# Three kinds of small extra products in the MLPs' first product, and one placement for all operands

## The chip, the cores and the metric

The kernel runs on one core of a Trainium2 chip. The number to predict is the device time of one execution, in microseconds (us). Engines are named as the profile does: PE is TensorE (PEld its weight loads), DVE is VectorE, ACT is ScalarE, POOL is GpSimd, SP is SyncE, which issues the weight DMAs. "Product" below is one matmul instruction.

## The reference

Three transformer-like layers over 256 tokens of width 1024, all in float32. The first block mixes three branches (a sparse attention, a gated recurrence, a short convolution); the second block has two layers, each with two kinds of attention. Every layer ends with the same kind of MLP:

```python
def squared_relu_mlp(h, w_up, w_down):
    return jnp.square(jax.nn.relu(h @ w_up)) @ w_down

x = x + squared_relu_mlp(rmsnorm(x, norm_mlp[layer]), w_up[layer], w_down[layer])
```

`w_up` is 1024 x 4096 and `w_down` 4096 x 1024, so an MLP's first product has 32 output tiles of 128 rows with 8 steps over the inner dimension. There are three MLPs: that of the first block, and one in each layer of the second.

## The kernel before, in words

Activations are kept transposed, features on partitions and the 256 tokens in the free dimension. A float32 product is made of three products in the one-pass type fp32r: weights and activations are each split into a high part and a rest, and high x high, high x rest and rest x high are added up in PSUM. The method `gemm` (lines 250, 253 and 254) issues these three for each step k, 128 x 128 weights stationary and 256 tokens moving. Weights come as one stream through SP; for each unit of 8 blocks ACT writes the high part `whi` (L193) and DVE the rest `wlo` in two pieces (L195).

The activations' two parts lie in one tile `xo`. Where they begin in it is set per stage by the table `PLACES`, in elements of 4 bytes; the tile itself begins at a multiple of 128 bytes plus 64. `HIDDEN` does the same for the MLP's hidden tile `hid`, which begins at a multiple of 128 bytes.

`residual` adds the last projection to x tile by tile (L375 on DVE), writes the next operand (L326 on ACT, L327 on DVE) and sums the squares of x on POOL (L339, L340) except the last, which ACT squares (L342). `mlp` begins with `variance`: two exact float32 products with a matrix of ones (`sum_squares`, L347 and L348) into the pool `po`, which has a single buffer, then a scaling by DVE that reads it (L382) and a reciprocal (L383). The mean square is not needed before the MLP's second product: the first product does not wait for it. In the first product each of 16 rounds makes two output tiles (`gemm2`: two calls of `gemm`, 24 products each); L395 to L398 make the squared ReLU. The second product runs mostly as pairs of one product of 512 columns and one of 256 (`gemm_wide`, L262 and L263), 7 tiles of 32 pairs for each MLP, and one last tile by `gemm`.

A scheduler orders each engine's instructions from the dependencies and its own estimates; the engines then run their queues in that order. `after(a, b)` adds an order between two instructions of one engine.

Of the kernel before, what the change touches and what calls it, by code (L numbers as in the profile page):

```python
# [10 lines left out]
FP32 = mybir.dt.float32  # L11
# [30 lines left out]


ROOM = 128
PLACES = {"block1": 32, "ln_mlp_g": 64, "norm_mix0": 24, "norm_mlp0": 96, "norm_mix1": 20, "norm_mlp1": 0}
HIDDEN = {"norm_mix0": 16, "norm_mix1": 48, None: 8}
MIXED = 16
HEADS = [16, 112]

# [33 lines left out]
def kernel(  # L83
# [11 lines left out]
    nc = tc.nc  # L95
    nosync = mybir.DependencyInfo(mybir.DependencyClass.NoSync, mybir.DependencyReason.DATA)

    def after(first, last):
        if last is not None:
            tc.add_manual_dep(first.ins, last.ins.name, nosync)  # L100

    def pool(name, bufs=1, space=None, stack=ctx):
        kw = {"space": space} if space is not None else {}
        return stack.enter_context(tc.tile_pool(name=name, bufs=bufs, **kw))
# [9 lines left out]
    po_p = pool("po", 1, PSUM)  # L114
# [7 lines left out]
    def placed(t, n, at):  # L122

        return t[:, at:at + n * T].rearrange("p (k t) -> p k t", k=n)

    def place(stage):

        nonlocal xh, xl
        at = PLACES[stage]
        xh, xl = placed(xo, KD, at), placed(xo, KD, at + KD * T)  # L130
# [3 lines left out]
    cst = keep.tile([128, NCONST], FP32, name="cst")  # L134
    ones = keep.tile([128, 128], FP32, name="ones")
# [10 lines left out]
    a = 0  # L146
    for k, cols in ((2, slice(0, FIRST)), (5, slice(FIRST, UW)), (8, slice(UW, CW))):
# [3 lines left out]
        a = e  # L151
# [16 lines left out]
    def v_(name, j=0):  # L168
        o = VOFF[name][0] + j
        return vec[:, o:o + 1]  # L170
# [5 lines left out]
    units = {}  # L176
# [6 lines left out]
    def take(u, pieces=2):  # L183

        c, i = divmod(u, CHUNK_UNITS)
        if c not in staged:
            load(c)
        src = staged[c][:, i * UW:(i + 1) * UW]
        h = whi_p.tile([128, UW], FP32R, name="whi")
        l = wlo_p.tile([128, UW], FP32R, name="wlo")  # L190
        n = UW // pieces
        pieces = [slice(q * n, (q + 1) * n) for q in range(pieces)]
        act = [nc.scalar.activation(out=h[:, z], in_=src[:, z], func=AF.Copy)  # L193
               for z in (pieces if u == 0 else [slice(0, UW)])]
        dve = [nc.vector.tensor_tensor(out=l[:, z], in0=src[:, z], in1=h[:, z], op=ALU.subtract) for z in pieces]  # L195
        chain = hold.pop(0) if hold else None
        if chain:
            after(act[0], chain[0])
            after(dve[0], chain[1])
        units.clear()  # L200
        units[u] = h, l

    def block(n=1):

        b = stream["block"]
        stream["block"] = b + n
        u, i = divmod(b, UNIT)
        assert i + n <= UNIT
        if u not in units:
            take(u)  # L210
        h, l = units[u]
        return h[:, i * 128:(i + n) * 128], l[:, i * 128:(i + n) * 128]
# [18 lines left out]
    def slot(steps=1):  # L231
        for d in list(due):
            d[0] -= 1
            if d[0] <= 0:
                due.remove(d)
                d[1]()
        credit[0] = credit[0] + steps if chains else 0
        while credit[0] >= 1:
            credit[0] -= 1
            step()  # L240

    def drain():
        while due or chains:
            slot()

    def gemm(ps, ks, ah, al, prev=None):

        for k in ks:
            h, l = block()
            m0 = nc.tensor.matmul(out=ps, lhsT=h, rhs=ah[:, k], start=(k == ks[0]), stop=False)  # L250
            if k == ks[0]:
                after(m0, prev)
            nc.tensor.matmul(out=ps, lhsT=h, rhs=al[:, k], start=False, stop=False)  # L253
            m1 = nc.tensor.matmul(out=ps, lhsT=l, rhs=ah[:, k], start=False, stop=(k == ks[-1]))  # L254
        return m1

    def gemm_wide(kt, a):

        ps = pg_p.tile([128, 2, T], FP32, name="pg")
        for k in range(kt):  # L260
            h, l = block()
            nc.tensor.matmul(out=ps, lhsT=h, rhs=a[:, k], start=(k == 0), stop=False)  # L262
            nc.tensor.matmul(out=ps[:, 1], lhsT=l, rhs=a[:, k, 0], start=False, stop=(k == kt - 1))  # L263
        slot(kt / KD)
        return ps

    def gemm1(kt, ah, al, steps=1):
        ks = kt if isinstance(kt, range) else range(kt)
        ps = pg_p.tile([128, 2, T], FP32, name="pg")
        gemm(ps[:, 0], ks, ah, al)  # L270
        slot(steps * len(ks) / KD)
        return ps[:, 0]

    def gemm2(kt, ah, al):
        ps = pg_p.tile([128, 2, T], FP32, name="pg")
        m = gemm(ps[:, 0], range(kt), ah, al)
        gemm(ps[:, 1], range(kt), ah, al, prev=m)
        slot(2 * kt / KD)
        return ps
# [44 lines left out]
    def operand(j, gain):  # L324

        nc.scalar.activation(out=xh[:, j], in_=x[:, j], func=AF.Copy, scale=v_(gain, j))  # L326
        nc.vector.scalar_tensor_tensor(out=xl[:, j], in0=x[:, j], scalar=v_(gain, j), in1=xh[:, j],  # L327
                                       op0=ALU.mult, op1=ALU.subtract)
# [16 lines left out]
    def sum_squares():  # L345
        ps = po_p.tile([128, 2, T], FP32, name="po")
        nc.tensor.matmul(out=ps[:, 0], lhsT=ones, rhs=sqa, start=True, stop=False)  # L347
        nc.tensor.matmul(out=ps[:, 0], lhsT=ones, rhs=sq_last["s"], start=False, stop=True)  # L348
        return ps[:, 0]
# [29 lines left out]
    def mlp(gain_next):  # L379
        def variance():  # L380
            u = tmp.tile([128, 512], FP32, name="rs_u", bufs=1)[:, 0:T]
            nc.vector.tensor_scalar(out=u, in0=sum_squares(), scalar1=1.0 / D, scalar2=EPS, op0=ALU.mult, op1=ALU.add)  # L382
            nc.vector.reciprocal(out=rvar, in_=u)  # L383

        variance()
        with ExitStack() as st:
            hp = pool("hid", stack=st)
            mp = pool("mlpt", 2, stack=st)
            hid = hp.tile([128, FF // 128 * 2 * T + ROOM], FP32R, name="hid")
            hid = placed(hid, FF // 128 * 2, HIDDEN[gain_next]).rearrange("p (k i) t -> p k i t", i=2)  # L390
            for j in range(0, FF // 128, 2):
                ps = gemm2(KD, xh, xl)
                r = mp.tile([128, 2, T], FP32, name="r")
                s = mp.tile([128, 2, T], FP32, name="s")
                nc.scalar.activation(out=r, in_=ps, func=AF.Relu)  # L395
                nc.scalar.activation(out=hid[:, j:j + 2, 0], in_=r, func=AF.Square)
                nc.vector.scalar_tensor_tensor(out=s, in0=ps, scalar=0.0, in1=r, op0=ALU.max, op1=ALU.mult)
                nc.vector.tensor_tensor(out=hid[:, j:j + 2, 1], in0=s, in1=hid[:, j:j + 2, 0], op=ALU.subtract)  # L398
            if gain_next is not None:
                place(gain_next)  # L400
            for j in range(KD):

                wide = j < KD - WN
                if wide:
                    ps = gemm_wide(FF // 128, hid)
                else:
                    ps = gemm1(FF // 128, hid[:, :, 0], hid[:, :, 1])

                for z in HALVES if gain_next is None and j == KD - 1 else [slice(0, T)]:
                    t = tmp.tile([128, T], FP32, name="dn")[:, z]  # L410
                    if wide:
                        nc.scalar.activation(out=t, in_=ps[:, 1], func=AF.Copy)
                        nc.vector.tensor_tensor(out=t, in0=ps[:, 0], in1=t, op=ALU.add)
                    nc.vector.tensor_tensor(out=t, in0=t if wide else ps[:, z], in1=rvar[:, z], op=ALU.mult)  # L414
                    nc.vector.tensor_tensor(out=x[:, j, z], in0=t, in1=x[:, j, z], op=ALU.add)  # L415
                    if z.stop - z.start < T:
                        nc.scalar.activation(out=rstd[:, z], in_=x[:, j, z], func=AF.Square)  # L417
                if gain_next is not None:
                    operand(j, gain_next)
                    squares(j)  # L420
                else:
                    if j < KD - 1:
                        squares(j)
                    nc.scalar.activation(out=xg[:, j], in_=x[:, j], func=AF.Copy, scale=v_("norm_final", j))  # L424
# [460 lines left out]
    for turn in (4096.0, 1.0):  # L885
# [4 lines left out]
        for i in range(6):  # L890
            m, e = math.frexp(rest)
# [14 lines left out]
    with ExitStack() as st:  # L906
# [82 lines left out]
        for j in range(0, 8, 2):  # L989
# [4 lines left out]
            qk(f"e{j + 1}")  # L994
        residual(oh, ol, GROUPS_ATT, "norm_mlp0")
    mlp("norm_mix1")


    first(rsqrt(sum_squares(), T, 1.0 / D, rstd))
    with ExitStack() as st:  # L1000
# [97 lines left out]
        a, b = rope(kr, 32)  # L1098
# [4 lines left out]
        for j in range(2):  # L1103
# [3 lines left out]
            a, b = rope(zr, 128)  # L1107
# [26 lines left out]
    room = pool("room").tile([128, 6, T // 2], FP32, name="room")  # L1134
# [213 lines left out]
```

## Time and profile before

| what | value |
|---|---|
| median of 2 runs | 1079.78 us (1079.7 to 1079.85) |
| the profiled execution's own time | 1079.46 us |
| its span, first to last instruction | 1077.7 us |
| PE busy | 1055.1 us, 98% of the span, 8136 products |
| DVE, ACT, POOL busy | 836.2, 602.0, 158.8 us |
| granted TensorE clock, mean | 0.998 |

An exact float32 product shows as two records of PE. Products are pipelined: each is shown some 0.28 us long while the next one starts after little more than a third of that, so what a product costs is read from the distance between starts, not from its length. A window's count includes products that were already running at its left edge.

### The profile page before, as it was taken

What the parts mean: (1) busy time and instruction counts of PE and PEld (TensorE: products, weight loads), DVE (VectorE), ACT (ScalarE), POOL (GpSimd) and SP (SyncE); (2) the same over time, 40 slices, a digit from 0 to 9 for tenths busy, and PEclk for the clock granted to TensorE, in tenths of its full rate; (3) what the DMA queues carried; (4) which work ended last, traced back from release to release, by engine and by line L of the source; (5) the groups of instructions that cost most, each with busy time, mean ns of one, the idle gap of its engine ahead of it and who ended that gap; (6) DMA issues with size and microseconds to landing.
All of it is one profiled execution on the core that took longest, in us unless ns stands there. A gap on an engine that the chain in (4) does not pass through costs nothing. (4 is left out here: it accounts for less than half of the span.)

```text
span 1077.7 us, 20317 instructions
## 1 busy us (share of the span) xinstructions
PE 1055.1 (98%) x8136; PEld 1015.3 (94%) x8136; DVE 836.2 (78%) x1613; ACT 602.0 (56%) x944; POOL 158.8 (15%) x174
## 2 busy tenths in 40 slices
PE   7999999999999999999999999999999999999996
PEld 7999989999999988899999999888999999999886
DVE  8999898887996666678778866667689788666663
ACT  6467456665575544456654655444458755555441
POOL 1045650110500001120003000011121022000110
PEclk9999999999999999999999999999999999999999
DMA  8544333545455555554433555554444334555541
GB/s 319 201 170 159 132 118 132 182 173 185 157 199 193 196 186 179 185 209 151 148 136 139 189 175 186 196 192 163 169 181 157 118 118 170 185 193 196 186 166 40
DMA packets 29007, 183.94 MB, mean 171 GB/s; under 512 B 3056, under 2 KB 6384, under 8 KB 7280
## 3 DMA queue, kind: packets, MB, share of 16 engines
q1 hardware_dynamic: 28768, 182.50, 47.5%
q8 instruction: 64, 1.05, 0.4%
q14 instruction: 31, 0.25, 0.1%
q10 hardware_dynamic: 144, 0.13, 0.0%
HBM read 181.57 MB, written 1.05 MB: 169 GB/s over the span
## 5 line engine op out<-in xcount | busy, mean ns | idle before, releaser
L195 DVE TENSOR_TENSOR wlo<-stg,whi 128x512 fp32r<-128x512 f32 (+1 forms) x676 | 470.8, 737 | 164.7 <-ACT whi L193 158.4
L193 ACT ACTIVATE whi<-stg 128x1024 fp32r<-128x1024 f32 (+1 forms) x340 | 356.0, 1050 | 333.8 <-PE pg L253 184.9
L250 PE MATMUL pg<-xo,whi 128*128 128x256 f32 x1472 | 415.7, 283 | 7.5 <-ACT whi L193 6.5
L254 PE MATMUL pg<-xo,wlo 128*128 128x256 f32 x1472 | 415.0, 282 | 0.4 <-DVE wlo L195 0.3
L253 PE MATMUL pg<-xo,whi 128*128 128x256 f32 x1472 | 414.4, 282 | 0.6 <-DVE xo L327 0.6
L250 PEld LDWEIGHTS pg<-xo,whi 128*128 128x128 f32 x1472 | 276.6, 188 | 8.9 <-ACT whi L193 6.8
L254 PEld LDWEIGHTS pg<-xo,wlo 128*128 128x128 f32 x1472 | 278.8, 190 | 1.7 <-DVE wlo L195 1.1
L253 PEld LDWEIGHTS pg<-xo,whi 128*128 128x128 f32 x1472 | 276.9, 188 | 2.1 <-DVE xo L327 1.3
L262 PE MATMUL pg<-hid,whi 128*128 128x512 f32 x672 | 235.1, 394 | 0.0
L263 PE MATMUL pg<-hid,wlo 128*128 128x256 f32 x672 | 188.9, 281 | 0.0
L262 PEld LDWEIGHTS pg<-hid,whi 128*128 128x128 f32 x672 | 126.3, 188 | 28.8
L263 PEld LDWEIGHTS pg<-hid,wlo 128*128 128x128 f32 x672 | 126.3, 188 | 0.0
L335 POOL TENSOR_TENSOR sqa<-xv 128x256 f32<-128x256 f32 x6 | 4.1, 677 | 468.3 <-DVE xv L415 302.8
L339 POOL TENSOR_TENSOR sq<-xv 128x256 f32<-128x256 f32 x36 | 28.3, 791 | 174.7 <-DVE xv L415 170.8
L289 PE MATMUL pg<-whi,xo 128*128 128x256 f32 x256 | 47.5, 283 | 0.0
L289 PEld LDWEIGHTS pg<-whi,xo 128*128 128x128 f32 x256 | 39.5, 188 | 0.1
L479 ACT ACTIVATE p<-p,m 128x128 f32<-128x128 f32 x64 | 28.6, 448 | 18.3 <-DVE m L477 18.3
L340 POOL TENSOR_TENSOR sqa<-sqa,sq 128x256 f32<-128x256 f32 x36 | 36.6, 1017 | 2.4
L253 PE MATMUL pg<-ol,whi 128*128 128x256 f32 x128 | 36.4, 286 | 0.2 <-DVE ol L299 0.2
L398 DVE TENSOR_TENSOR hid<-s,hid 128x512 fp32r<-128x512 f32 x48 | 33.2, 691 | 4.0
L254 PE MATMUL pg<-oh,wlo 128*128 128x256 f32 x128 | 36.1, 285 | 0.0
L289 PE MATMUL pg<-wlo,xo 128*128 128x256 f32 x128 | 36.0, 281 | 0.0
(356 smaller groups left out, 1540.1 us busy)
## 6 DMA issues: line engine op xcount, KB each, us to landing
stg<-w SPq DMA_DIRECT2D x168, 1024.0 KB, 4.8
t<-t_bias SPq DMA_DIRECT2D x8, 128.0 KB, 2.5
cb<-chk_bias SPq DMA_DIRECT2D x1, 1024.0 KB, 4.8
xv<-x_in SPq DMA_DIRECT2D x2, 384.0 KB, 5.9
cst<-consts SPq DMA_DIRECT2D x1, 640.0 KB, 10.6
stg<-w SPq DMA_DIRECT2D x1, 512.0 KB, 7.7
out<-xg SPq DMA_DIRECT2D x2, 256.0 KB, 2.5
stg<-w SPq DMA_DIRECT2D x1, 384.0 KB, 6.4
```

The source lines that it names most:

```text
L193: act = [nc.scalar.activation(out=h[:, z], in_=src[:, z], func=AF.Copy) for z in (pieces if u == 0 else [slice(0, UW)])]
L195: dve = [nc.vector.tensor_tensor(out=l[:, z], in0=src[:, z], in1=h[:, z], op=ALU.subtract) for z in pieces]
L250: m0 = nc.tensor.matmul(out=ps, lhsT=h, rhs=ah[:, k], start=(k == ks[0]), stop=False)
L253: nc.tensor.matmul(out=ps, lhsT=h, rhs=al[:, k], start=False, stop=False)
L254: m1 = nc.tensor.matmul(out=ps, lhsT=l, rhs=ah[:, k], start=False, stop=(k == ks[-1]))
L262: nc.tensor.matmul(out=ps, lhsT=h, rhs=a[:, k], start=(k == 0), stop=False)
L263: nc.tensor.matmul(out=ps[:, 1], lhsT=l, rhs=a[:, k, 0], start=False, stop=(k == kt - 1))
L289: nc.tensor.matmul(out=ps, lhsT=a[:, k, t], rhs=w_, start=(k == 0 and i == 0), stop=(k == kt - 1 and i == 2))
L339: nc.gpsimd.tensor_tensor(out=s, in0=x[:, j], in1=x[:, j], op=ALU.mult)
L340: nc.gpsimd.tensor_tensor(out=sqa, in0=sqa, in1=s, op=ALU.add)
L398: nc.vector.tensor_tensor(out=hid[:, j:j + 2, 1], in0=s, in1=hid[:, j:j + 2, 0], op=ALU.subtract)
L479: nc.scalar.activation(out=p[:, a:b], in_=p[:, a:b], func=AF.Exp, scale=-1.0, bias=m[:, i:i + 1], accum_out=sums[:, i:i + 1])
```

## The change

Before the first step of each of the 32 calls of `gemm` in an MLP's first product, one to three extra products are issued into a tile of the pool `po`, whose result nobody reads. Their kind depends on the MLP. In the first ("tokens") the activations are stationary and n columns of weights move; 8 entries in turn, 11 products, so 44 in all. In the second ("dense") the weights are stationary and n tokens move: 32 products. In the third ("exact") ones and constants in plain float32: 32 products. All of `PLACES` becomes 32 and all of `HIDDEN` 8, so that `xo` operands begin 64 bytes past a multiple of 128 in every stage (they did in four of six) and `hid` 32 bytes past one (it did in the third MLP, and 64 past it in the first two).

```diff
-PLACES = {"block1": 32, "ln_mlp_g": 64, "norm_mix0": 24, "norm_mlp0": 96, "norm_mix1": 20, "norm_mlp1": 0}
-HIDDEN = {"norm_mix0": 16, "norm_mix1": 48, None: 8}
+PLACES = {"block1": 32, "ln_mlp_g": 32, "norm_mix0": 32, "norm_mlp0": 32, "norm_mix1": 32, "norm_mlp1": 32}
+HIDDEN = {"norm_mix0": 8, "norm_mix1": 8, None: 8}
+
+BETWEEN = {
+    "norm_mix0": [("tokens", 256), ("tokens", 256, 2), ("tokens", 128), ("tokens", 256, 3),
+                  ("tokens", 240), ("tokens", 200), ("tokens", 248), ("tokens", 136)],
+    "norm_mix1": [("dense", n) for n in (72, 88, 104, 120, 100, 68, 84, 92, 76, 108, 116, 124, 136, 152, 8, 24)],
+    None: [("exact", n) for n in (1, 16, 64, 100, 128, 200, 248, 256)],
+}
...
+    between = {"list": [], "n": 0, "room": None}
+
+    def small(ah, prev):
+
+        kind, n, times = (between["list"][between["n"] % len(between["list"])] + (1,))[:3]
+        between["n"] += 1
+        h = next(iter(units.values()))[0]
+        for _ in range(times):
+            a, b = {"tokens": (ah[:, 0, 0:128], h[:, 0:n]), "dense": (h[:, 0:128], ah[:, 0, 0:n]),
+                    "exact": (ones, cst[:, 0:n])}[kind]
+            m = nc.tensor.matmul(out=between["room"][:, 0:n], lhsT=a, rhs=b, start=True, stop=True)
+            after(m, prev)
+            prev = m
+        return prev
+
     def gemm(ps, ks, ah, al, prev=None):
 
         for k in ks:
             h, l = block()
+            if k == ks[0] and between["list"]:
+                prev = small(ah, prev)
             m0 = nc.tensor.matmul(out=ps, lhsT=h, rhs=ah[:, k], start=(k == ks[0]), stop=False)
             if k == ks[0]:
                 after(m0, prev)
...
+            between.update(list=BETWEEN[gain_next], n=0, room=po_p.tile([128, 512], FP32, name="po"))
             for j in range(0, FF // 128, 2):
                 ps = gemm2(KD, xh, xl)
...
+            between["list"] = []
```

The extra lines also move what follows: lines ahead of 250 are 7 higher in the changed kernel (L195 becomes L202), later ones 24 to 26 (L250, L253, L254 become L274, L277, L278; L327, L375 become L351, L399; L347, L348 become L371, L372; L382, L383 become L406, L407; the extra product is L263).

PE at the start of the second MLP, before. `oh`, `ol` are the operands of the last residual tile, `xo` those of the MLP's first product:

```order
L250 MATMUL pg<-oh,whi 128x256
L253 MATMUL pg<-ol,whi 128x256
L254 MATMUL pg<-oh,wlo 128x256
L250 MATMUL pg<-xo,whi 128x256
L253 MATMUL pg<-xo,whi 128x256
L254 MATMUL pg<-xo,wlo 128x256
```

The MLP's first tile follows the residual's last tile directly. The two sums of squares stand some 70 rows further on, among later tiles of the same product:

```order
L250 MATMUL pg<-xo,whi 128x256
L253 MATMUL pg<-xo,whi 128x256
L347 MATMUL po<-sqa,ones 128x256
L348 MATMUL po<-sq,ones 128x256
L254 MATMUL pg<-xo,wlo 128x256
```

The same place in the changed kernel, with what each waits for left out:

```order
L274 MATMUL pg<-oh,whi 128x256
L277 MATMUL pg<-ol,whi 128x256
L278 MATMUL pg<-oh,wlo 128x256
L371 MATMUL po<-sqa,ones 128x256
L372 MATMUL po<-sq,ones 128x256
L263 MATMUL po<-xo,whi 128x72
L274 MATMUL pg<-xo,whi 128x256
```

The extra product needs the buffer of `po`, so both sums of squares, and DVE's read of them, now stand ahead of the first tile; it stands so in all three MLPs.

DVE at the same place, before (L327 are the rests of the operand, L195 the weights' rests):

```order
L375 TENSOR_TENSOR xv<-pg,xv 128x256
L195 TENSOR_TENSOR wlo<-stg,whi 128x512 x2
L327 SCALAR_TENSOR_TENSOR xo<-xv,xo 128x256 x3
L195 TENSOR_TENSOR wlo<-stg,whi 128x512 x2
L382 TENSOR_SCALAR rs_u<-po 128x256
L383 RECIPROCAL rvar<-rs_u 128x256
```

And in the changed kernel:

```order
L399 TENSOR_TENSOR xv<-pg,xv 128x256
L202 TENSOR_TENSOR wlo<-stg,whi 128x512 x2
L351 SCALAR_TENSOR_TENSOR xo<-xv,xo 128x256 x3
L406 TENSOR_SCALAR rs_u<-po 128x256
L407 RECIPROCAL rvar<-rs_u 128x256
```

The read of the sums moves one pair of L195 forward; what stands ahead of it is unchanged. In the first MLP the order up to the read is that of before, with the angle arithmetic of L884 to L899 behind it.

## Rows read from the trace of the kernel before

**Rows 1.** The page's first part: busy time, share of the span, instructions of PE.

```profile
PE 1055.1 (98%) x8136; PEld 1015.3 (94%) x8136; DVE 836.2 (78%) x1613; ACT 602.0 (56%) x944; POOL 158.8 (15%) x174
```

**Rows 2.** Stretches: window, length, busy time (xcount) of each engine, PEclk, DMA share, GB/s.

```profile
32.00:46.00 14.00, 14.00 (x126) 14.00 (x126) 14.00 (x47) 5.66 (x6) 0.00 (x0) 1.00 0.56 202
290.00:360.00 70.00, 70.00 (x597) 70.00 (x596) 55.47 (x99) 44.05 (x55) 0.00 (x0) 1.00 0.56 196
384.00:450.00 66.00, 66.00 (x380) 57.81 (x379) 44.51 (x71) 29.46 (x36) 9.00 (x11) 1.00 0.54 192
686.00:752.00 66.00, 66.00 (x376) 57.29 (x375) 43.77 (x71) 28.43 (x35) 8.96 (x11) 1.00 0.52 188
986.00:1050.00 64.00, 64.00 (x371) 56.72 (x371) 40.73 (x65) 28.61 (x35) 8.49 (x10) 1.00 0.51 181
```

**Rows 3.** Timeline of PE around exact products: start, length, engine, line, operation.

```profile
289.19 0.59 PE L348 MATMUL po<-sq,ones 128*128 128x256 f32 x2
289.43 0.47 PE L250 MATMUL pg<-xo,whi 128*128 128x256 f32 x1
289.73 0.28 PE L253 MATMUL pg<-xo,whi 128*128 128x256 f32 x1
...
475.51 0.50 PE L360 MATMUL sc<-cst,rstd 128*128 128x1 f32 x4
475.87 0.49 PE L289 MATMUL pg<-whi,xo 128*128 128x256 f32 x2
476.19 0.28 PE L289 MATMUL pg<-wlo,xo 128*128 128x256 f32 x1
```

**Rows 4.** Timeline at the first MLP's start, PE, ACT and DVE.

```profile
283.50 0.29 PE L254 MATMUL pg<-mh,wlo 128*128 128x256 f32 x1
...
288.54 0.40 ACT L342 ACTIVATE sq<-xv 128x256 f32<-128x256 f32 x1
...
289.81 0.34 DVE L884 TENSOR_SCALAR sq<-sq,xv 128x256 f32<-128x256 f32 x1
```

**Rows 5.** Timeline at the second MLP's start, PE, DVE and POOL.

```profile
585.57 0.28 PE L254 MATMUL pg<-oh,wlo 128*128 128x256 f32 x1
...
591.88 2.59 DVE L327 SCALAR_TENSOR_TENSOR xo<-xv,xo 128x256 fp32r<-128x256 f32 x3
...
592.40 1.79 POOL L340 TENSOR_TENSOR sqa<-sqa,sq 128x256 f32<-128x256 f32 x2
```

**Rows 6.** Timeline at the third MLP's start, PE and POOL.

```profile
886.18 0.28 PE L254 MATMUL pg<-oh,wlo 128*128 128x256 f32 x1
...
892.63 2.06 POOL L340 TENSOR_TENSOR sqa<-sqa,sq 128x256 f32<-128x256 f32 x2
```

**Rows 7.** Stretches, instructions of `xo` alone: PE, PEld, DVE, ACT, clock, DMA.

```profile
283.63:290.60 6.97, 6.18 (x46) 5.58 (x47) 2.27 (x4) 1.02 (x2) 1.00 0.51 162
585.69:595.70 10.01, 9.25 (x72) 8.78 (x73) 5.34 (x7) 1.53 (x3) 1.00 0.29 105
886.30:896.15 9.85, 9.24 (x73) 8.74 (x74) 5.54 (x7) 1.52 (x4) 1.00 0.18 57
```

**Rows 8.** The end: PE's last product, and two stretches (columns as Rows 2).

```profile
1069.35 0.39 PE L1145 MATMUL sc<-rstd,ones 128*128 128x128 f32 x2
...
1069.80:1073.00 3.20, 0.00 (x0) 0.00 (x0) 3.05 (x12) 0.77 (x4) 0.00 (x0) 1.00 0.00 0
1073.00:1074.00 1.00, 0.00 (x0) 0.00 (x0) 1.00 (x2) 0.00 (x0) 0.00 (x0) 0.77 0.85 257
```

**Rows 9.** Timeline of PE at the kernel's start.

```profile
5.01 0.58 PE L250 MATMUL pg<-xo,whi 128*128 128x256 f32 x1 [5.01 <-ACT whi L193]
...
11.42 0.41 PE L250 MATMUL pg<-xo,whi 128*128 128x256 f32 x1
11.63 0.41 PE L253 MATMUL pg<-xo,whi 128*128 128x256 f32 x1
...
12.04 0.28 PE L250 MATMUL pg<-xo,whi 128*128 128x256 f32 x1
```

## Prediction

> **What bounds the kernel.** I read the busy shares first: PE works in 98% of the span, so the time is PE's stream of products plus its few idle places, and whatever is put into that stream or holds it up is paid in full [rows 1]. Then stretches, to see what a product costs: in the first MLP's first product 70 us hold 597 products; two were already running at the left edge, so one starts every 70/595 = 0.1176 us [rows 2]. The reader should see in the same rows that this spacing isn't fixed: an early stretch of the first block, with the same product at the same offset, gives 14.00/124 = 0.1129 us. The second products show it too. A pair (512 and 256 columns) takes 66/189 = 0.3492 us in the first MLP, 66/187 = 0.3529 in the second, both with `hid` at 64 bytes, and 64/184.5 = 0.3469 in the third, at 32. The granted clock is 1.00 in all five. So there are at least two paces at 64 bytes. Last I read timelines where the changed kernel has a new order: the three starts of an MLP [rows 4 to 6].
>
> **Extra products.** The exact kind has rows. From the start of L348 to that of the second product behind it 0.54 us pass, less one ordinary 0.118: an exact product of 256 columns costs 0.422 us [rows 3]. Two of one column (L360, four records) and two ordinary ones take 476.19 - 475.51 = 0.68 us; less 2 x 0.118 that is 0.444, so 0.222 for one, 0.111 for a record: a floor, whatever the width. I take the larger of 0.222 and 0.422 x n/256. The eight widths then cost 5 x 0.222 + 0.330 + 0.409 + 0.422 = 2.27 us, four times over **9.1 us**.
>
> Of fp32r no row shows fewer than 256 columns. 24 of the "tokens" products have 256 and cost 24 x 0.118 = 2.8 us. The other 20, and all 32 "dense" ones, cost at least a record's floor, 52 x 0.111 = 5.8 us. At most they run at the exact type's rate of 0.422/256 = 1.65 ns a column: the 20 have 4 x 952 columns, 6.3 us, and the dense ones, with the floor under the two narrowest, 5.2 us, together 11.5. The fp32r row alone speaks for the low end; but that these products are narrow is just what no row covers, so I take the middle, 8.6 us. All 108 products: 9.1 + 2.8 + 8.6 = **20.5 us**, between 17.7 and 23.4. None is hidden: PE is full around each of them.
>
> **The start of each MLP.** The extra products' buffer comes from the pool `po`, which has one. It is free once VectorE has read the sums of squares (L382, now L406), so in PE's queue both sums and that read stand ahead of the MLP's first tile. Before, PE worked on tiles in this time. Behind the waiting product the whole first product is queued, and PE has nothing else.
>
> When can PE go on? In the second MLP, POOL's last addition ends at 592.40 + 1.79 = 594.19; VectorE's last operand at 591.88 + 2.59 = 594.47, which is in time [rows 5]. The two sums follow: the second starts 0.42 later and runs 0.59 as L348 did [rows 3], to 595.2; the read takes about 0.4 (an estimate from the 0.34 of a VectorE operation of the same width [rows 4]). PE goes on near 595.7, having finished the residual at 585.57 + 0.28 = 585.85 [rows 5]. In the third MLP POOL ends at 894.69, so PE goes on near 896.15, after 886.46 [rows 6]. In the first MLP ScalarE's square ends at 288.94, and the sum is over near 289.6; but VectorE first works through L884, to 290.15, so PE goes on near 290.6, after 283.79 [rows 4].
>
> The loss is the tile work done before in these windows: 46, 72 and 73 products [rows 7], at 0.1176 us 5.4, 8.5 and 8.6 us. In the second and third windows the kernel before had not yet run its two sums (2 x 0.42 = 0.84); the changed one has, so 0.84 comes off each. Net 5.4 + 7.6 + 7.7 = **20.8 us** (18.5 to 23). Nothing gives it back: ScalarE and VectorE get ahead, but PE wasn't waiting for them. This work gets no cover elsewhere.
>
> **The clock.** After PE's last product, over at 1069.74, the granted clock is still 1.00 until 1073 and 0.77 as a mean of the next microsecond [rows 8]: it fell to its lower level (1.2 of 2.4 GHz) some 3.7 us after work ended. The new gaps before the sums in the second and third MLP are 594.19 - 585.85 = 8.3 and 894.69 - 886.46 = 8.2 us, so it will fall there. At the low level products start 0.21 us apart (11.63 less 11.42), and at the kernel's start it took from 5.01 to about 11.85 until they got short [rows 9]. So each of the two gaps costs 0.84 for sums at half pace, and up to 4.5 us of products at 0.21 instead of 0.118, up to 2.0 us. I take 1.0 of it: 2 x 1.84 = **3.7 us**. The first MLP's gap is broken after 3.1 us by the first sum, and I put 0 there. Ends: 0 (no fall) and 7.7 (all three in full).
>
> **Paces.** Every extra product disturbs the stream, and behind it a tile of 24 may run at the slow pace or the fast one. All three first products, 3 x 768 = 2,304 products, at the fast pace would give back 2,304 x 4.7 ns = 10.8 us; the other end is 0. No row says which follows a disturbance; I take a quarter, **-2.7 us**. The second products' `hid` at 32 bytes should run like the third MLP's: 224 pairs x (2.3 + 6.0) ns = 1.9 us; since 64 bytes has two paces, 32 may have a slower one too (3.7 ns a pair, as at 64), which would make it +0.6. I take **-1.5**. Some 1,030 products of the two attention layers move from other offsets to 64: by the two paces between -4.8 and +1; I take **-0.5**.
>
> Against these terms stands a rule of the Trainium skill, "TensorE: Matmul & The Clock Gate", in "Step-by-step: what each phase is for": PE has two independent read ports into SBUF, so loading the next weights takes nothing from the running product. By it offsets should not matter, and the sum would be 4.7 us higher. The trace doesn't agree with it as a full account, since pace differs at one clock and one width [rows 2]; whether the ports cause that no row shows.
>
> **Sum.** 20.5 + 20.8 + 3.7 - 2.7 - 1.5 - 0.5 = 40.3. The profiled execution took 1079.46, so 1119.8; the median of the runs is 0.3 higher: **1120 us**, 3.7% slower. The order in which the remaining VectorE work stands (the angle arithmetic comes earlier in the first MLP, L195 later by one pair elsewhere) I cost at nothing: five buffers for each part of the weights let ScalarE and VectorE run ahead of PE. If that cover is gone, a late unit costs PE a wait of at most one unit, 24 products or 2.8 us.
>
> **Rivals.**
> - *Fast pace everywhere.* Each extra product resets the stream to the fast pace. For: both paces occur at 64 bytes. Against: the slow one held through 597 products. It gives 10.8 - 2.7 = 8 us more and up to 4 from the attention layers: 1108 to 1112. Chance 0.12.
> - *No change of pace, or a longer low clock.* Tiles keep 0.1176, as the rule on the ports would have it, so the 4.7 us aren't earned: 1125; with the clock's upper end 1129. For: long constant stretches. Against: rows 2. Chance 0.15.
> - *Not slower by what can be told: the sums are early.* If POOL and VectorE were done when PE reaches the MLP, the buffer would be free and the starts would cost nothing. The terms of 20.8 and 3.7 go, and 1095.5 is left, 1.5% up. It decides at the residual's last product: the sums must be ready by 585.85, but POOL ends 8.3 us later [rows 5] and PE's wait does not speed it up. Chance 0.04.
> - *The change doesn't do what it says.* The products' results aren't read, but nothing in the queue drops them: they stand there, 108 rows more. Under 0.01.
>
> **How the numbers follow.** The forecast itself has 0.68. Its own spread (products +-2.9, starts +-2, clock -3.7 to +4) is about 1113 to 1127; the fast rival pulls the low end to 1107, the slow one the high end to 1130, and that range leaves out some 2 in 10. "Faster" and "slower" mean by over 2%, which is about what a measurement can tell from no change: below 1058 or above 1101. Only the third rival is within: same 0.04, with 0.01 for faster; the rest, 0.95, is slower.
>
> **What would show it.** Three idle stretches of PE at the MLPs' starts, 7 to 10 us with the sums inside, ended by the read at L406; low clock behind at least two of them; L263 with 44, 32 and 32 products; second products at 0.347 a pair. In the first products, the spacing between two extra ones tells the share of fast tiles. I am wrong in the mechanism if PE starts the MLP within 2 us of the residual's end, and in a size if the narrow products cost outside 0.11 to 0.25 us (dense), or the clock stays at 1.00.

## The result, and the profile after

The changed kernel takes **1126.09 us** (1124.84 to 1127.33, two runs), 1.0432 times the time before, interval 1.0409 to 1.0455. Forecast were 1120 us and 1107 to 1130. The profiled execution took 1124.84 us, 45.4 more than that of before.

The first part of the page after, PE's row as [rows 1]; under it, from the page's second part, PE's busy tenths and the granted clock in 40 slices of 28 us:

```profile
PE 1080.1 (96%) x8276; PEld 1040.6 (93%) x8276; DVE 841.7 (75%) x1613; ACT 603.1 (54%) x944; POOL 157.5 (14%) x174
...
PE   7999999999899999999996999999999969999996
...
PEclk9999999999899999999998999999999979999999
```

PE has 140 rows more (108 products, of which the 32 exact ones show as two records each), 25 us more work, and 20 us more idle time. The idle time isn't spread: the slices that hold the starts of the three MLPs (the 11th, the 22nd, the 33rd) fall, and the clock falls in them.

PE's longest waits after (engine, line, what it waited for, us in total, times, longest). Before, the second row had a counterpart of 6.5 us (twice, the kernel's start) and the first one of 0.3 us (once):

```profile
PE po L371 <- POOL sqa L364: 19.5, 3, 8.2
PE pg L274 <- ACT whi L200: 6.8, 2, 5.0
...
PE po L263 <- DVE rs_u L406: 1.6, 3, 0.5
PE po L372 <- ACT sq L366: 1.4, 1, 1.4
```

Three new waits, once in each MLP, 22.5 us together: the first sum of squares waits for POOL's last addition (L364), in one MLP the second sum waits for ScalarE's square, and the extra product for VectorE's read of the sums. PE's timeline at the first two starts, to lay beside [rows 4] and [rows 5] (in brackets: idle time before, and what ended it):

```profile
284.34 0.28 PE L278 MATMUL pg<-mh,wlo 128*128 128x256 f32 x1
287.68 0.70 PE L371 MATMUL po<-sqa,ones 128*128 128x256 f32 x2 [3.06 <-POOL sqa L364]
289.81 1.22 PE L372 MATMUL po<-sq,ones 128*128 128x256 f32 x2 [1.43 <-ACT sq L366]
291.55 0.58 PE L263 MATMUL po<-whi,xo 128*128 128x256 f32 x1 [0.52 <-DVE rs_u L406]
...
597.75 0.28 PE L278 MATMUL pg<-oh,wlo 128*128 128x256 f32 x1
606.27 1.22 PE L371 MATMUL po<-sqa,ones 128*128 128x256 f32 x2 [8.24 <-POOL sqa L364]
607.28 1.06 PE L372 MATMUL po<-sq,ones 128*128 128x256 f32 x2
608.86 0.43 PE L263 MATMUL po<-xo,whi 128*128 128x72 f32 x1 [0.52 <-DVE rs_u L406]
609.10 0.56 PE L274 MATMUL pg<-xo,whi 128*128 128x256 f32 x1
```

The second sum at 289.81 takes 1.22 us and not the 0.59 of [rows 3]: the clock had fallen. The stretches of low clock (columns as in [rows 2]: window, length, busy time and count of PE, PEld, DVE, ACT, POOL, PEclk, DMA share, GB/s):

```profile
289.30:296.12 6.82, 5.79 (x23) 5.08 (x24) 6.52 (x15) 0.46 (x2) 0.00 (x0) 0.50 0.42 154
603.32:613.56 10.24, 6.77 (x26) 5.88 (x27) 5.36 (x6) 0.42 (x1) 2.82 (x4) 0.50 0.00 0
913.93:927.59 13.66, 7.54 (x29) 6.64 (x30) 8.01 (x10) 0.93 (x2) 5.39 (x7) 0.50 0.21 77
```

All three starts have one. The clock falls before PE goes on and stays at 1.2 GHz for 4.6, 4.7 and 5.5 us of tile work behind it.

For the rest I cut both traces into the same stages: from the last residual product to the MLP's first `pg<-xo` product ("start"), the first product, the second product. Differences after less before, in us:

| | first MLP | second | third | sum |
|---|---|---|---|---|
| start | 7.59 - 0.12 | 11.35 - 0.12 | 11.52 - 0.12 | +30.1 |
| first product | 96.89 - 92.09 | 96.03 - 92.86 | 101.76 - 92.57 | +17.2 |
| second product | 88.74 - 89.35 | 88.74 - 90.33 | 88.74 - 88.75 | -2.2 |

The attention layers add -0.4 and the stretch up to the first residual's end +0.8: +45.5 in all.

### The profile page after: what moved, and what is told of

Its sections match the earlier page's. It is cut to its first block, busy times and chain, and to the rows that moved or that the text cites. A ratio compares the mean times of both kernels' runs of the same rounds, so it can differ in the third digit from the quotient of the medians.

```text
span 1123.1 us, 20595 instructions
## 1 busy us (share of the span) xinstructions
PE 1080.1 (96%) x8276; PEld 1040.6 (93%) x8276; DVE 841.7 (75%) x1613; ACT 603.1 (54%) x944; POOL 157.5 (14%) x174
## 3 DMA queue, kind: packets, MB, share of 16 engines
q1 hardware_dynamic: 28768, 182.50, 45.5%
## 4 chain that ended last, share of the span: by engine, by line
PE 69%; POOL 2%; ACT 1%; DVE 1%; issue 0%; DVEq 0%; POOLq 0%
PE pg L286 14%; PE pg L274 13%; PE pg L277 13%; PE pg L278 13%; PE pg L287 7%; PE pg L313 3%; PE po L263 1%; PE po L522 1%; PE sc L485 1%; POOL sqa L364 1%; PE pt L515 1%; POOL sq L363 1%; PE sc L478 1%; PE po L523 1%; ACT whi L200 0%; PE po L372 0%
## 5 line engine op out<-in xcount | busy, mean ns | idle before, releaser
L202 DVE TENSOR_TENSOR wlo<-stg,whi 128x512 fp32r<-128x512 f32 (+1 forms) x676 | 473.4, 742 | 199.7 <-ACT whi L200 197.5
L274 PE MATMUL pg<-xo,whi 128*128 128x256 f32 x1472 | 425.3, 289 | 7.2 <-ACT whi L200 6.8
L277 PE MATMUL pg<-xo,whi 128*128 128x256 f32 x1472 | 417.1, 283 | 0.1
L278 PE MATMUL pg<-xo,wlo 128*128 128x256 f32 x1472 | 416.5, 283 | 0.2 <-DVE wlo L202 0.2
L274 PEld LDWEIGHTS pg<-xo,whi 128*128 128x128 f32 x1472 | 280.3, 190 | 8.4 <-ACT whi L200 7.1
L277 PEld LDWEIGHTS pg<-xo,whi 128*128 128x128 f32 x1472 | 280.5, 191 | 1.1 <-DVE xo L351 0.4
L278 PEld LDWEIGHTS pg<-xo,wlo 128*128 128x128 f32 x1472 | 280.0, 190 | 0.9 <-DVE wlo L202 0.4
L364 POOL TENSOR_TENSOR sqa<-sqa,sq 128x256 f32<-128x256 f32 x36 | 36.4, 1012 | 2.3
L277 PE MATMUL pg<-ol,whi 128*128 128x256 f32 x128 | 36.4, 286 | 0.2 <-DVE ol L323 0.2
L278 PE MATMUL pg<-oh,wlo 128*128 128x256 f32 x128 | 36.1, 285 | 0.0
```

Source lines behind the costliest of these rows:

```text
L364: nc.gpsimd.tensor_tensor(out=sqa, in0=sqa, in1=s, op=ALU.add)
```

## Experiments

Each was run beside the kernel before, whose median was 1077.15, 1077.56, 1078.28 and 1077.69 us in four groups of runs (beside the ninth stands a single one of 1080.80); its single runs spread over 5 to 7 us in each group, so small differences are read from stages of the traces rather than from medians. Stage times below are cut as in the table above. "Own buffer" means that the extra products' tile comes from the pool `pt`, which the sums of squares don't use.

**1. The products without the wait for the sums' buffer.**

```diff
-between.update(..., room=po_p.tile([128, 512], FP32, name="po"))
+between.update(..., room=pt_p.tile([128, 512], FP32, name="pt"))
```

> All 108 extra products stay, but their tile comes from the pool of the attention's transposes, which is idle in the MLPs, so that they need not wait for the sums of squares. Theory (the buffer's wait at the three starts, with the low clock behind it, is some 30 us of the 46): 1094 to 1098 us, no idle stretch of PE over 1.5 us at an MLP's start, granted clock 1.00 throughout. Rival (the products in the stream cost the time, by their number or by disturbing it, and the wait only moved work about): 1115 us or more.

Measured 1112.53, ratio 1.0316 (1.0292 to 1.0339). It fell between both expectations: the wait for the sums is gone, but more than half of its cost came back. PE's waits, and its timeline in the second MLP:

```profile
PE pg L277 <- DVE xo L351: 7.1, 8, 2.3
...
PE po L371 <- POOL sqa L364: 0.7, 1, 0.7
```

```profile
594.44 0.28 PE L274 MATMUL pg<-xo,whi 128*128 128x256 f32 x1
595.66 0.39 PE L277 MATMUL pg<-xo,whi 128*128 128x256 f32 x1 [0.94 <-DVE xo L351]
...
598.63 0.41 PE L274 MATMUL pg<-xo,whi 128*128 128x256 f32 x1
600.94 0.58 PE L277 MATMUL pg<-xo,whi 128*128 128x256 f32 x1 [1.89 <-DVE xo L351]
```

PE now stops inside the first tile, step by step, each time for the rest of the operand that VectorE is writing (L351). In the kernel before, the scheduler had interleaved tiles of several rounds there, so that each operand step that arrived fed several of them. The extra products all write one tile and here run in the program's order, and that of a pair's second call is tied behind the first call by `after`; so the first tile must be through before any other begins, and the interleaving is gone. (That the one tile is what ties the rounds is read from the code; extra products with a tile each weren't run.) The clock falls too, in a window with the columns as above:

```profile
597.40:607.60 10.20, 8.24 (x34) 7.34 (x34) 6.51 (x9) 1.98 (x3) 4.78 (x6) 0.50 0.25 81
```

A second wait had been hidden behind the first.

**2. The wait without the products:** only the first extra product of each MLP.

```diff
-            if k == ks[0] and between["list"]:
+            if k == ks[0] and between["list"] and between["n"] == 0:
```

> Only the first extra product of each MLP is left, 3 of 108, in the buffer of the sums of squares as in the change. Theory (105 products cost 17.4 us in the trace of the changed kernel, the fast tiles behind the triple products give 0.4): 1108 to 1111 us, with the three idle stretches and the low clock as in the change. Rival (the products are the cost): 1080 to 1083 us.

Measured 1109.56, ratio 1.0298 (1.0272 to 1.0325). Three products carry two thirds of the loss. The waits are those of the changed kernel:

```profile
PE po L371 <- POOL sqa L364: 19.6, 3, 8.3
...
PE po L263 <- DVE rs_u L406: 1.6, 3, 0.5
PE po L372 <- ACT sq L366: 1.4, 1, 1.4
```

**3. The placement alone:** the kernel before with the new `PLACES` and `HIDDEN`.

```diff
+PLACES = {"block1": 32, "ln_mlp_g": 32, "norm_mix0": 32, "norm_mlp0": 32, "norm_mix1": 32, "norm_mlp1": 32}
+HIDDEN = {"norm_mix0": 8, "norm_mix1": 8, None: 8}
```

> The kernel before with the new placement of operands alone, no extra product. Theory (the second products run at 0.3466 us a pair in all three MLPs, nothing else changes by more than 0.5 us): 1077.0 to 1077.8 us. Rival (the pace of a stage is drawn anew by any change, so the second products may as well get slower): 1079 to 1082 us.

Measured 1078.51, ratio 1.0007 (0.9996 to 1.0017): between both expectations, and no gain in the median. The stages do show it. The second products, as windows (columns as above):

```profile
384.00:448.00 64.00, 64.00 (x372) 56.72 (x371) 43.01 (x70) 28.42 (x35) 7.88 (x10) 1.00 0.52 184
686.00:750.00 64.00, 64.00 (x371) 56.74 (x370) 43.23 (x70) 28.51 (x35) 7.96 (x10) 1.00 0.53 195
986.00:1050.00 64.00, 64.00 (x371) 56.72 (x371) 41.21 (x64) 28.76 (x36) 9.56 (x11) 1.00 0.50 181
```

All three hold as many products as the third MLP did before [rows 2], and last 88.74 us each: 2.2 us less in all. But the stretch up to the first residual's end took 284.8 us, against 283.5 and 284.2 in two traces of the kernel before; in the other traces it lies between 284.1 and 286.1 without any change to it. Why the medians don't show the 2.2 us I leave open; both traces of the kernel before are of its longer runs (experiments 7 and 8).

**4. The wait with PE kept busy:** useless products of 256 columns (25 in the first MLP, 62 in the others) between the residual and the sums, in their own buffer.

```diff
+            for _ in range(fill):
+                m = nc.tensor.matmul(out=room[:, 0:T], lhsT=filler["h"], rhs=xh[:, 0], start=True, stop=True)
+                after(m, prev)
+                prev = m
-        nc.tensor.matmul(out=ps[:, 0], lhsT=ones, rhs=sqa, start=True, stop=False)
+        m = nc.tensor.matmul(out=ps[:, 0], lhsT=ones, rhs=sqa, start=True, stop=False)
+        after(m, prev)
```

> The change with useless products of 256 columns put into the idle stretches ahead of the sums of squares (25 in the first MLP, 62 in each of the others), none longer than the wait. PE starts the MLPs no earlier, but is busy until the sums. Theory (the low clock behind the idle stretches costs some 8 us): 1117 to 1120 us, granted clock 1.00 at the second and third start; at the first it may still fall between the sums. Rival (the wait is the whole cost and the lower clock costs next to nothing, since the products behind it are bound elsewhere): 1125 to 1127 us.

Measured 1116.80, ratio 1.0363 (1.0340 to 1.0386). The added work makes the kernel faster than the change itself. Windows:

```profile
293.00:296.40 3.40, 3.40 (x18) 3.40 (x18) 2.86 (x4) 0.00 (x0) 0.00 (x0) 0.50 0.51 161
598.00:606.00 8.00, 7.58 (x63) 7.35 (x63) 6.14 (x11) 2.68 (x5) 7.37 (x9) 1.00 0.41 133
909.00:920.00 11.00, 9.99 (x80) 9.34 (x79) 8.11 (x13) 2.45 (x4) 6.08 (x8) 1.00 0.09 14
```

In the second and third MLP the clock stays at 1.00, and start and first product together take 3.6 and 3.8 us less than in the change. In the first MLP it still falls, later and for half as long, and only 0.5 us come back. Part of the first MLP's share is hidden by VectorE: with the added products the scheduler put more of the angle arithmetic ahead of its read, which began 0.7 us after the second sum's end (290.84):

```profile
291.54 0.42 DVE L419 TENSOR_SCALAR rs_u<-po 128x256 f32<-128x256 f32 x1
```

So the low clock costs 7.9 us at least; the rest of the start is the wait.

**5. Own buffer, and no extra product in the first six calls of each MLP** (26 of 32 calls keep theirs).

```diff
-            if k == ks[0] and between["list"]:
+            between["calls"] += k == ks[0]
+            if k == ks[0] and between["list"] and between["calls"] > 6:
```

> As the run with the extra products in their own buffer, but the first 6 calls of each first product carry none (26 of 32 do), so that the scheduler may again interleave the first three pairs of tiles while their operand arrives. Theory (that run's 34 us were 17 of products and some 15 of a second wait: the extra products write one tile in program order and so tie the first tiles into a row, each step waiting for its operand): about 14 us above the kernel before, 1091 to 1094, no wait of PE for the operand over 1 us and the clock at 1.00. Rival (the products slow the stream around them, wherever they stand): 28 us or more above it.

Measured 1092.84, ratio 1.0133 (1.0116 to 1.0151). The two traces' spans differ by 1111.4 - 1090.6 = 20.8 us between experiments 1 and 5. Each list starts at the seventh call, so its last entries are left out: eight products of "tokens", six "dense", and exact ones of 64, 100, 128, 200, 248 and 256 columns, about 3.4 us at the costs below. The other 17.4 are the lost interleaving and the clock behind it. What remains over experiment 3, 14.3 us, is the price of the products that are left (14.4 by the costs below).

**6. One group of three "tokens" products ahead of the 8th call,** own buffer, placement as in the change.

```diff
-between.update(list=BETWEEN[gain_next], n=0, ...)
+between.update(list=[("tokens", 256, 3)], n=0, calls=0, ...)
...
+            if k == ks[0] and between["list"] and between["calls"] == 8:
```

> The new placement, and one triple extra product of the tokens kind (256 columns) per MLP, ahead of the eighth call, in its own buffer. Theory (in the changed kernel the four tiles behind such a triple, and no others, ran at 0.1133 us a product; a pace stays until something disturbs the stream): the 25 calls from there on run at 0.1133, 600 products x 4.5 ns = 2.7 us less 0.35 for the triple, in each MLP, 7 us less than with the placement alone, 1070 to 1073 us. Rival (each tile's own change of PSUM buffer sets the pace back): 1078 to 1081 us.

Measured 1077.67, ratio 0.9993 (0.9982 to 1.0004): near the rival's time, but not for its reason, since in the first MLP the new pace held over many tiles. Windows in the first products of the three MLPs:

```profile
320.00:370.00 50.00, 50.00 (x443) 50.00 (x442) 37.35 (x59) 30.11 (x37) 0.00 (x0) 1.00 0.56 197
625.00:675.00 50.00, 50.00 (x427) 50.00 (x426) 34.16 (x54) 28.57 (x36) 0.00 (x0) 1.00 0.52 182
918.00:968.00 50.00, 50.00 (x427) 50.00 (x426) 34.16 (x53) 28.96 (x36) 0.00 (x0) 1.00 0.53 190
```

Two of the products were running at the left edge: 50/441 = 0.1134 us in the first MLP, 50/425 = 0.1176 in the others. One group switched the first MLP to the fast pace for the rest of its first product, and did nothing in the other two.

**7 and 8. The kernel before and the change, once more.**

> The kernel before once more, for its paces in another execution. Theory (the pace of a stage at 64 bytes follows from what stands ahead of it): the second products of the first two MLPs at 0.349 and 0.353 us a pair as in the first profile, within 0.2 us in all. Rival (the pace is drawn anew in each execution where the offset allows two): another spacing in at least one of the six long stages, and a span up to 4 us away.

> The changed kernel on this chip, beside the others. 1123 to 1127 us; the two theories agree. The spread of its runs shows how much the low clock's end behind the three starts moves from one execution to the next.

Measured 1080.15 and 1125.39 (ratio 1.0434, 1.0413 to 1.0456). Every stage of the kernel before behind the first residual is within 0.04 us of the first trace, so in these two executions its paces are the same. That it is so in every execution is not shown: of its 63 single times beside the experiments 42 lie between 1074.8 and 1078.5 us, 21 between 1079.5 and 1081.5 and none in the gap, and both traces (1079.46 and 1080.15) go with the longer ones. In the change's second trace the clock fell 2.7, 2.3 and 2.9 us after the residual's last product and stayed low for 10.2, 13.7 and 13.7 us, so where it falls and for how long moves between executions.

**9. Groups of 1, 2, 3, 4, 5 and 6 products** ahead of the 8th, 11th, 14th, 17th, 20th and 23rd call.

```diff
+    list=[("tokens", 256, m) for m in range(1, 7)]
...
+    between["calls"] in (8, 11, 14, 17, 20, 23)
```

> The new placement; the extra products in a buffer of their own, and only ahead of six calls of each MLP (the 8th, 11th, 14th, 17th, 20th and 23rd): 1, 2, 3, 4, 5 and 6 products of 256 columns. In e6 one group of three put the first MLP on the fast pace for good (0.1133 us a product in place of 0.1178) and left the other two MLPs on the slow one. If the pace behind a group depends on where in the stream's cycle of three lines the group falls, and so on its number, some counts switch the second and third MLP too, and others switch the first one back: the pace changes at some of the six places and is kept between them. If only a group of three in the first MLP does it, the pace changes at most there. Cost: 21 products an MLP, 2.5 us, 7.4 in all; with no switch 1080 + 7.4 - 2 = 1085, each MLP at the fast pace over half of its tiles gives back 1.2 to 1.8.

Measured 1081.84 (one run). In all three MLPs alike the products behind the groups of 1, 2, 4 and 5 start 0.1178 us apart, and those behind the groups of 3 and 6 0.1133: from three in a row it goes to the fast pace, from four back to the slow one, behind five it stays there, and from six it is fast again.

**10, 11 and 12. Groups of 1, 2 and 3 ahead of the 8th, 9th and 10th call; one group of 6 ahead of the 8th; groups of 1 and 3 ahead of the 8th and 9th.** The edit of the tenth; the other two differ in the two lists:

```diff
+    list=[("tokens", 256, m) for m in (1, 2, 3)]
...
+    between["calls"] in (8, 9, 10)
```

> The new placement; the extra products in a buffer of their own, and only ahead of the 8th, 9th and 10th call of each MLP: 1, 2 and 3 products of 256 columns. In e9 groups of 1, 2 and 3, 72 products apart, put all three MLPs on the fast pace (0.1133 us a product), until the next group took them off it. If the number of products put in is what decides, the same three groups 24 apart do it too, and the pace holds to the end of the first product: 22 calls x 24 x 4.5 ns = 2.4 us less 6 x 0.118 = 0.7, so 1.7 us an MLP, 5 in all, and 2 more by the placement: 1072 to 1074 beside 1077 to 1080 for the kernel before. If the distance between the groups or their place matters, the second and third MLP stay at 0.1178 as in e6, and the time is that of e6, 1077 to 1080.

> As e10, but one group of 6 products ahead of the 8th call. In e9 the group of 6 put all three MLPs on the fast pace behind a slow stretch. If the number in the group decides, it does so here: 24 calls x 24 x 4.5 ns = 2.6 less 0.7, 1.9 us an MLP: 1071 to 1074. If what was put in before counts too, some MLP stays slow, as behind e6's single group of 3: 1075 to 1080.

> As e10, but only two groups: 1 product ahead of the 8th call of each MLP and 3 ahead of the 9th. If a group of three (or six) switches to the fast pace wherever some other group stood ahead of it in the same MLP, all three MLPs run at 0.1133 from the 9th call on: 23 calls x 24 x 4.5 ns = 2.5 less 4 x 0.118 = 0.5, so 2.0 us an MLP; 1071 to 1074, as e10 or up to 1 us below it. If it takes the particular sum of 1 and 2 (e9, e10), the second and third MLP stay at 0.1178 and the time is that of e6 and e11, near 1077.

Measured 1073.07 (ratio 0.9952, 0.9934 to 0.9969), 1077.67 (0.9991, 0.9979 to 1.0003) and 1077.18 (0.9997, 0.9986 to 1.0007). Windows of the tenth:

```profile
320.00:370.00 50.00, 50.00 (x444) 50.00 (x443) 37.09 (x58) 30.52 (x38) 0.00 (x0) 1.00 0.55 193
625.00:675.00 50.00, 50.00 (x444) 50.00 (x443) 35.88 (x56) 30.22 (x37) 0.00 (x0) 1.00 0.54 198
918.00:968.00 50.00, 50.00 (x444) 50.00 (x443) 35.95 (x56) 29.22 (x36) 0.00 (x0) 1.00 0.54 197
```

All three MLPs are fast: their first products take 90.4 to 91.0 us against 92.1 to 92.9 before. The eleventh and twelfth read like the sixth, with one fast MLP and two slow ones. The tenth beats both kernels, by 0.5% over the kernel before, an interval clear of 1. What makes a group take in the second and third MLP is left open: behind groups of 1 and 2 three do, alone or behind a single 1 they don't, nor do six alone.

## Why the prediction was nearly right

**The mechanism was right.** The buffer of `po` holds PE at each MLP's start until POOL's last addition, the sums and VectorE's read are done. In the second MLP PE was to go on 10.1 us after the start of its last residual product (595.7 - 585.57 [rows 5]); it went on after 608.86 - 597.75 = 11.1. In the first MLP it went on 6.9 us after the residual's end (291.55 - 284.62), for 6.8 forecast. There L910 (before: L884) stands ahead of VectorE's read in the trace, as the prediction had it, and not behind it as the section on the change says:

```profile
290.63 0.34 DVE L910 TENSOR_SCALAR sq<-sq,xv 128x256 f32<-128x256 f32 x1
291.07 0.42 DVE L406 TENSOR_SCALAR rs_u<-po 128x256 f32<-128x256 f32 x1
```

Experiment 2 shows the start to be two thirds of the loss, and experiment 5 the products to be the other third.

**The clock was sized too small; this is the step that failed most.** The starts had 20.8 us and the clock 3.7, 24.5 together. Experiment 2 against experiment 3 measures both: start and first product take 7.7, 11.5 and 11.9 us more, 31.1, of which the three products are some 0.45; that leaves 7.6, 11.4 and 11.7, or 30.6. The forecast had 5.4, 9.4 and 9.5: every start is about 2 too low. The wait itself was sized right: with the gaps filled (experiment 4) the second and third MLP's start and first product take 10.9 and 16.7 us more than in experiment 3, less 3.6 and 9.2 for the products that is 7.3 and 7.5, against 7.6 and 7.7 forecast. The rest is the clock. For the first MLP I put 0, arguing that the first sum breaks the gap; it cost about 2.2 (7.6 less 5.4), since PE went on there when it was forecast to. The sum did not save the clock: the sum ran from 287.68 to 288.38, and the clock fell at 289.30, 4.7 us after the residual's last product had ended (284.62). In the other two I took half of the slow products. In fact sums ran at half pace and products lay 0.213 us apart for 4.7 and 5.5 us; experiment 4 gives 3.6 and 3.8 back there, more than the upper end that I gave, 2.84 an MLP. The clock cost 9.6 in all (2.2 + 3.6 + 3.8), not 3.7.

**The extra products were sized too large.** From the trace after, the cost read as in [rows 3], from one product ahead to the second behind, less two ordinary ones:

```profile
652.10 0.28 PE L278 MATMUL pg<-xo,wlo 128*128 128x256 f32 x1
652.22 0.17 PE L263 MATMUL po<-xo,whi 128*128 128x8 f32 x1
652.25 0.37 PE L274 MATMUL pg<-xo,whi 128*128 128x256 f32 x1
652.45 0.28 PE L277 MATMUL pg<-xo,whi 128*128 128x256 f32 x1
...
946.23 0.28 PE L278 MATMUL pg<-xo,wlo 128*128 128x256 f32 x1
946.34 0.59 PE L263 MATMUL po<-cst,ones 128*128 128x256 f32 x2
946.58 0.47 PE L274 MATMUL pg<-xo,whi 128*128 128x256 f32 x1
946.89 0.28 PE L277 MATMUL pg<-xo,whi 128*128 128x256 f32 x1
...
949.48 0.28 PE L278 MATMUL pg<-xo,wlo 128*128 128x256 f32 x1
949.60 0.28 PE L263 MATMUL po<-cst,ones 128*128 128x1 f32 x2
949.73 0.36 PE L274 MATMUL pg<-xo,whi 128*128 128x256 f32 x1
949.93 0.28 PE L277 MATMUL pg<-xo,whi 128*128 128x256 f32 x1
```

An exact product of 256 columns costs 0.66 - 0.236 = 0.42 us and one of one column 0.45 - 0.236 = 0.21: the exact term, 9.1, was right (9.2 measured). An fp32r product of 8 columns costs 0.35 - 0.236 = 0.11, and all dense ones from 8 to 152 columns between 0.108 and 0.114. The narrow ones together take some 5.8 us, not the middle value 8.6; that they would run at the exact type's rate per column was a bound that I should have given little weight, since the one fp32r row stood at the other end. All 108 cost 17.8.

The Trainium skill's page "TensorE: Matmul & The Clock Gate", section "LDWEIGHTS (loading the stationary operand)", states that loading weights takes, in ns, the number of weight columns over 1.2; nothing of the product's width is in it. For 128 columns that makes 107 ns (an estimate), and each product here has such a load. The trace agrees: 0.108 to 0.114 us from 8 columns to 152. By it the narrow term would have been 5.6 (an estimate, 52 x 0.107).

**The paces were sized too large.** I took a quarter of 10.8 us. Only the four tiles behind a group of three (at 302.64, 326.4, 350.2 and 374.0) ran fast, and the next single product took the pace back; all others at the high clock kept 0.1177 to 0.1180:

```profile
302.64 0.52 PE L263 MATMUL po<-whi,xo 128*128 128x256 f32 x3
302.99 0.28 PE L274 MATMUL pg<-xo,whi 128*128 128x256 f32 x1
...
305.60 0.28 PE L278 MATMUL pg<-xo,wlo 128*128 128x256 f32 x1
305.71 0.27 PE L263 MATMUL po<-whi,xo 128*128 128x240 f32 x1
```

From 302.99 to 305.60 there are 23 steps of 0.1135 us. Four tiles of 24 give 0.4 us instead of 2.7.

**The second products and the rest were right.** In the changed kernel too they last 88.74 us in each MLP, 2.2 us less in all than in the trace of before (forecast -1.5), and the attention layers give 0.4 (0.5). The reordered VectorE work cost nothing that shows.

Against the profiled execution the terms missed by +6.1 (starts and clock), -2.7 (products), +2.3 (paces), -0.7 (second products), +0.1 (attention) and +0.8 (the stretch ahead of the first MLP, which had no term): 5.9 together, where the time missed by 5.0 (1124.84 - 1119.8). The rest is mainly that the low clock of experiment 2, from which the first term is read, lasted a little longer than that of the profiled execution. That the products stayed 2.7 below their term and so hid part of the clock's miss is luck. Of the rival with no change of pace or a longer low clock, 1125 to 1129, the clock's half came about beyond its upper end, and in the first products the pace's half; the second products did earn their term. The one with early sums fell: PE did wait 8.2 us for POOL. The fast pace everywhere exists, but it takes particular groups of products ahead (experiment 10).

What I did not see is the second wait behind the first. With a buffer of its own the change would still have cost 35 us: a forecast of that kernel by the sum above, 1095, would have been 17 too low.

## What to carry to other kernels

Before something is put into the stream of the busiest engine, ask whose buffer it takes and which order it brings: a tile that several steps write kept those steps in program order here, and so undid an interleaving that hid late operands. The gaps in PE's work cost more than themselves here, since the clock fell in them and stayed low for about 5 us of the work behind; useless products in the gap paid. Narrow fp32r products weren't cheaper here for being narrow: from 8 to 152 columns each cost 0.108 to 0.114 us.

## What was not expected of the hardware

- **Two paces that a few products switch.** The same products, at one clock and one offset, start 0.1133 or 0.1178 us apart, and stay so for hundreds of products. Two executions of the kernel before agree in it (experiment 7); whether all do is open. Groups of 1, 2, 4 and 5 extra products always left or put it on the slow one, groups of 3 and 6 could put it on the fast one (experiments 6 and 9 to 12).
- **The clock fell in spite of a sum in the middle of the gap.** In the profiled execution it fell 4.7, 5.3 and 2.6 us after the residual's last product at the three starts, and in that of before 3.8 us after the kernel's last product [rows 8]; at the first start a sum of 0.7 us in between did not prevent it.
- **It fell without a long gap too.** In experiment 1 it was low from 597.4 on, when PE had been at the second MLP's first tile since 594.09 and no wait there had been longer than 0.94 us.
